# A macaron trunk in hi/lo fp32: the seven-product scheme moved from the down projection to gate and up

## The chip, the cores and the metric

One core of one Trainium2 chip runs the whole network in one program. The metric is the device time of one execution in microseconds, the median of three runs. Engines by their names in the profile: PE (matmul), ACT, DVE, POOL, and SP, which issues the DMAs.

## The reference, cut to what matters

```python
T, D, DFF = 512, 1024, 2816
def _swiglu(x, w_in, w_out):
    gate, up = jnp.split(x @ w_in, 2, axis=-1)
    return (jax.nn.silu(gate) * up) @ w_out
...
for layer in range(2):
    x = x + 0.5 * _swiglu(_rmsnorm(x, ffn1_norm[layer]), ffn1_w_in[layer], ffn1_w_out[layer])
    x = x + mixer(_rmsnorm(x, mix_norm[layer]))
    x = x + 0.5 * _swiglu(_rmsnorm(x, ffn2_norm[layer]), ffn2_w_in[layer], ffn2_w_out[layer])
return _rmsnorm(x, final_norm)
```

The mixer of layer 0 is a convolution beside sparse attention, that of layer 1 a short convolution beside stick-breaking attention. The change does not touch the mixers. Four FFNs (the `_swiglu` lines) are what it is about.

## The kernel before, in words

Tokens stay on chip as `xT`, 8 tiles of 128 channels x 512 tokens. Every fp32 operand is cut in two fp32r parts by `split`: ACT copies it to the high half, DVE subtracts to get the low half. `mm3` then makes three matmuls of each product: high weight by high tokens (L120), high weight by low tokens (L121), low weight by high tokens (L122). So PE cannot begin a weight before ACT's part is done, and its third matmul waits for DVE's. A weight tile is 128 x 1024; `load_w` brings it by one DMA of 512 KB, and the halves go to the pools `whi` and `wlo` with three slots each.

In an FFN, DFF is 22 blocks of 128. `up(s)` computes the gate and up projections of two blocks directly: four weights, 24 matmuls of 512 columns each into banks `gu`. The tokens are not normed ahead (the gain is in them, L94); DVE multiplies gate (L263) and up (L266) by `rstd`, ACT takes Silu, DVE multiplies both (L270). `rstd` itself is made while the first projections run: PE sums squares (`rs`, L187), DVE takes the inverse root, PE spreads it over the partitions (`rb`, L208), ACT copies it (L209).

`seven` is a scheme of seven block products in place of eight (Winograd's form of Strassen's). The 2 x 2 blocks are weights 11, 12, 21, 22 and the token operand in 2 x 2 blocks, with 256 token columns in a block. Sums of weight blocks come from DVE, sums of token blocks from DVE once per operand (`Seven`). In the kernel before, the down projection of 18 blocks goes this way: three groups of three pairs, two halves of the output channels each, that is six sevens per FFN of 7 x 18 matmuls of 256 columns. The products 11, T2, T1 and 22 add up in bank X (`px`), 12 in Y (`py`), T3 and T4 in W (`pw`), and after each product DVE adds the bank to `xT` (L285). The other four blocks go the direct way at the end (`down_tail`, 96 matmuls of 512 columns).

Order: each engine runs its instructions in a fixed order which a scheduler made when the kernel was built, and waits on semaphores. Names below end in numbers that count tiles.

Of the kernel before, what the change touches and what calls it, by code (L numbers as in the profile page):

```python
# [34 lines left out]
S_11, S_21, S_22, S_T1, S_T3, S_T2, S_T4 = 1, 2, 3, 4, 5, 6, 7  # L35


CHUNKS = [3, 3, 3]
TAIL = NP - 2 * sum(CHUNKS)

# [12 lines left out]
def trunk(ctx: ExitStack, tc: tile.TileContext, a: dict, out: bass.AP):  # L53
# [71 lines left out]
    def halves(t):  # L125
        return t.rearrange("p (s t) -> p s t", t=TH)

    def sums(e, b, t):

        x = [b[:, i * TH:(i + 1) * TH] for i in range(4)]  # L130
        y = [t[:, i * TH:(i + 1) * TH] for i in range(4)]
        e.tensor_tensor(y[0], x[1], x[0], ALU.subtract)
        e.tensor_tensor(y[1], x[3], x[0], ALU.subtract)
        e.tensor_tensor(y[2], x[3], y[0], ALU.add)
        e.tensor_tensor(y[3], y[2], x[2], ALU.subtract)

    class Seven:


        def __init__(self, hi, lo, b, t, e):  # L140
            self.hi, self.lo = hi, lo
            sums(e, b, t)
            split(hi[:, :3 * TH], lo[:, :3 * TH], b[:, TH:])
            split(hi[:, 3 * TH:], lo[:, 3 * TH:], t)

        def __getitem__(self, s):
            sl = slice((s - 1) * TH, s * TH)
            return self.hi[:, sl], self.lo[:, sl]


    class Norm:
        def __init__(self, col):
            self.col, self.h, self.l, self.ss, self.order = col, {}, {}, [], []

        def operand(self, k):
            hi = xnp.tile([P, T], F32R, tag="xn", name=nm("xh"))
            lo = xnp.tile([P, T], F32R, tag="xn", name=nm("xl"))
            split(hi, lo, xT[:, k, :], prm[:, self.col + k:self.col + k + 1])
            self.h[k], self.l[k] = hi, lo
            self.order.append(k)  # L160

        def square(self, k):
            sq = cp.tile([P, T], F32, tag="c", name=nm("sq"))
            S.activation(sq, xT[:, k, :], AF.Square)  # L164
            self.n = len(self.ss) and self.n + 1
            if not self.ss:
                self.ss = [sq]
            else:
                s2 = cp.tile([P, T], F32, tag="c", name=nm("ss"))
                (V if self.n == KD - 1 else G).tensor_tensor(s2, self.ss[0], sq, ALU.add)  # L170
                self.ss = [s2]
# [40 lines left out]
    def seven(ph, blocks, n, ops, taps):  # L212

        w = 2 * n * P
        raw = {}
        for b in ("11", "12", "22", "21"):
            raw[b] = ph.tile("rb", "rb", 768)[:, :w]
            nc.sync.dma_start(raw[b], blocks[b])  # L220
        s = {i: ph.tile("ws", "ws", 768)[:, :w] for i in (1, 2)}
        X, Y, W = (ph.bank(t, t) for t in ("px", "py", "pw"))

        def product(name, o, src, op, first, sign=None):
            hi = wsp.tile([P, 1024], F32R, tag="whi", name=nm("whi"))[:, :w]
            lo = wsp.tile([P, 1024], F32R, tag="wlo", name=nm("wlo"))[:, :w]
            split(hi, lo, src, sign)
            for k in range(n):
                for j in range(2):
                    sl = slice((j * n + k) * P, (j * n + k + 1) * P)  # L230
                    mm3(o[:, j * TH:(j + 1) * TH], hi[:, sl], lo[:, sl], *ops[k][op],
                        first and k == 0 and j == 0, k == n - 1, skip_group_check=True)
            taps(name, o)

        product("1", X, raw["11"], S_11, True)
        product("2", Y, raw["12"], S_21, True)
        V.tensor_tensor(s[1], raw["21"], raw["22"], ALU.add)
        V.tensor_tensor(s[2], s[1], raw["11"], ALU.add)
        product("6", X, s[2], S_T2, False, -1.0)
        V.tensor_tensor(raw["21"], raw["11"], raw["21"], ALU.add)  # L240
        product("7", W, raw["21"], S_T3, True)
        product("5", X, s[1], S_T1, False)
        product("4", W, raw["22"], S_T4, False)
        V.tensor_tensor(s[2], s[2], raw["12"], ALU.add)
        product("3", X, s[2], S_22, False)

    def ffn(norm, w_in, w_out, w_tail, nxt, ph, last=None):
        act = {}

        def up(s):  # L250

            blk = ph.wide("hb")
            for r in range(2):
                ps = []
                for gu in range(2):
                    hi, lo = load_w(w_in[2 * s + r, :, gu], KD * P)
                    o = ph.bank("gu")
                    for i, k in enumerate(norm.order):
                        sl = slice(k * P, (k + 1) * P)
                        mm3(o, hi[:, sl], lo[:, sl], norm.h[k], norm.l[k], i == 0, i == KD - 1)  # L260
                    ps.append(o)
                g = ph.tile("g")
                V.tensor_tensor(g, ps[0], rstd, ALU.mult)  # L263
                S.activation(g, g, AF.Silu)
                u = ph.tile("u")
                V.tensor_tensor(u, ps[1], rstd, ALU.mult)  # L266

                o = halves(blk)[:, 2 * r:2 * r + 2]
                tail = s >= sum(CHUNKS)
                V.tensor_tensor(o if r or tail else o[:, ::-1], halves(g), halves(u), ALU.mult)  # L270
            if tail:
                h, l = (ph.rtile("at", "act", 1792) for _ in range(2))
                split(h[:, :1024], l[:, :1024], blk)
                act[s] = [(h[:, r * T:(r + 1) * T], l[:, r * T:(r + 1) * T]) for r in range(2)]
                return
            act[s] = Seven(ph.rtile("ah", "act", 1792), ph.rtile("al", "act", 1792), blk, ph.wide("ht"), V)

        def down(c0, n, q):

            m0 = 4 * q  # L280

            def taps(m, o):
                r, c = {"1": (0, 0), "2": (0, 0), "6": (1, 0), "7": (1, 1), "5": (1, 1), "4": (1, 0), "3": (0, 1)}[m]
                x = xT[:, m0 + 2 * r:m0 + 2 * r + 2, c * TH:(c + 1) * TH]
                V.scalar_tensor_tensor(x, halves(o), -0.5 if r else 0.5, x, op0=ALU.mult, op1=ALU.add)  # L285

            w = 2 * n * P
            blocks = {b: w_out[q, i, :, 2 * c0 * P:2 * c0 * P + w] for i, b in enumerate(("11", "21", "12", "22"))}
            seven(ph, blocks, n, [act[c0 + k] for k in range(n)], taps)

        done = 0
        for i, n in enumerate(CHUNKS):
            c0 = sum(CHUNKS[:i])

            while done < min(c0 + n + 1, NP // 2):
                up(done)
                done += 1
            for q in range(2):
                down(c0, n, q)
                if done < NP // 2 and q == 0:  # L300
                    up(done)
                    done += 1

        ops = sum([act[s] for s in range(sum(CHUNKS), NP // 2)], [])
        ws = {}

        def down_tail(m, ts):
            o = ph.bank("fo")[:, ts]
            if m // 2 not in ws:
                ws[m // 2] = load_w(w_tail[m // 2], 2 * TAIL * P)  # L310
            hi, lo = ws[m // 2]
            for k in range(TAIL):
                sl = slice((m % 2 * TAIL + k) * P, (m % 2 * TAIL + k + 1) * P)
                mm3(o, hi[:, sl], lo[:, sl], ops[k][0][:, ts], ops[k][1][:, ts], k == 0, k == TAIL - 1)
            V.scalar_tensor_tensor(xT[:, m, ts], o, 0.5, xT[:, m, ts], op0=ALU.mult, op1=ALU.add)
# [20 lines left out]
    class Phase:  # L336
# [706 lines left out]
```

## Time and profile before

| | us |
|---|---|
| median of 3 runs | 1965.54 (1963.14 to 1967.5) |
| profiled execution | 1965.56 |
| its span in the trace | 1963.8 |
| mean granted clock of PE | 0.994 |

The profile is of one execution. Its span is 1.8 us shorter than the time of that execution, and that execution is within 0.1 us of the median, so rows of the trace can be added to the time directly.

### The profile page before, as it was taken

The page shows a single profiled execution, that of the slowest core. Times are in us where ns is not written, and L with a number is a line of the kernel's source. Part 1 is how long each engine was busy: PE and PEld are TensorE (multiplying, and loading weights), DVE is VectorE, ACT ScalarE, POOL GpSimd, SP SyncE. Part 2 cuts the span into 40 slices and gives each one's busy share as a digit, 9 for nine tenths or more (in the row PEclk, how much of TensorE's full clock was granted, in tenths as well). Part 3 has the DMA queues.
Part 4 walks back from the last instruction along what each step waited for, and adds up shares of the span by engine and source line. Part 5 has one row for each costly group of instructions (what it writes and reads, how often), then busy time and mean ns, then how long its engine had stood idle before and what let it go on. Part 6 is the DMA issues. An engine that isn't in the chain of part 4 may idle for free.

```text
span 1963.8 us, 25263 instructions
## 1 busy us (share of the span) xinstructions
PE 1930.6 (98%) x10128; PEld 1632.0 (83%) x10128; DVE 1322.0 (67%) x1973; ACT 790.1 (40%) x1129; POOL 104.1 (5%) x112
## 2 busy tenths in 40 slices
PE   8999999989999999999999999999999999999997
PEld 6888989878667888888988888888877888888896
DVE  6566757699986656666675666656578655666664
ACT  5333323436685433333343333334545433333333
POOL 2000000100232100000010000001000110000001
PEclk9999999999999999999999999999999999999999
DMA  6233331332100432323233333322321243232311
GB/s 220 94 91 102 92 102 52 100 103 82 43 1 28 150 97 84 113 82 117 86 111 96 97 97 98 98 80 75 94 67 55 77 143 97 84 114 81 117 52 54
DMA packets 53972, 178.02 MB, mean 91 GB/s; under 512 B 5984, under 2 KB 6368, under 8 KB 53856
## 3 DMA queue, kind: packets, MB, share of 16 engines
q1 hardware_dynamic: 53712, 176.29, 28.7%
q8 instruction: 79, 1.29, 0.3%
q14 instruction: 37, 0.30, 0.0%
q10 hardware_dynamic: 144, 0.14, 0.0%
HBM read 174.30 MB, written 2.10 MB: 90 GB/s over the span
## 4 chain that ended last, share of the span: by engine, by line
PE 97%; DVE 1%; ACT 1%; issue 0%; DMA 0%; DVEq 0%; SPq 0%; ACTq 0%
PE gu L120 16%; PE gu L121 16%; PE gu L122 16%; PE px L120 4%; PE px L122 4%; PE px L121 4%; PE ac L120 3%; PE ac L122 3%; PE ac L121 3%; PE pw L122 2%; PE pw L121 2%; PE pw L120 2%; PE fo L120 2%; PE fo L121 2%; PE fo L122 2%; PE mo L121 1%
## 5 line engine op out<-in xcount | busy, mean ns | idle before, releaser
L120 PE MATMUL gu<-xh,whi 128*128 128x512 f32 x1408 | 549.7, 391 | 8.3 <-ACT whi L90 6.1
L121 PE MATMUL gu<-xl,whi 128*128 128x512 f32 x1408 | 549.9, 391 | 0.0
L122 PE MATMUL gu<-xh,wlo 128*128 128x512 f32 x1408 | 546.4, 390 | 0.0
L90 ACT ACTIVATE whi<-raw 128x1024 fp32r<-128x1024 f32 (+2 forms) x256 | 268.9, 1051 | 565.3 <-PE gu L121 188.7
L91 DVE TENSOR_TENSOR wlo<-raw,whi 128x1024 fp32r<-128x1024 f32 (+2 forms) x256 | 312.8, 1222 | 55.0 <-ACT whi L90 51.0
L120 PEld LDWEIGHTS gu<-xh,whi 128*128 128x128 f32 x1408 | 265.5, 189 | 62.6 <-ACT whi L90 6.3
L122 PEld LDWEIGHTS gu<-xh,wlo 128*128 128x128 f32 x1408 | 265.2, 188 | 55.4
L121 PEld LDWEIGHTS gu<-xl,whi 128*128 128x128 f32 x1408 | 265.4, 189 | 53.8
L266 DVE TENSOR_TENSOR u<-gu,rstd 128x512 f32<-128x512 f32 x88 | 60.8, 691 | 264.6 <-PE gu L122 264.6
L90 ACT ACTIVATE whi<-rb 128x768 fp32r<-128x768 f32 x96 | 81.4, 848 | 266.5 <-PE gu L121 166.3
L263 DVE TENSOR_TENSOR g<-gu,rstd 128x512 f32<-128x512 f32 x88 | 60.8, 691 | 162.3 <-PE gu L122 155.8
L120 PE MATMUL px<-ah,whi 128*128 128x256 f32 x576 | 165.4, 287 | 1.6
L122 PE MATMUL px<-ah,wlo 128*128 128x256 f32 x576 | 163.4, 284 | 0.0
L121 PE MATMUL px<-al,whi 128*128 128x256 f32 x576 | 162.7, 282 | 0.0
L120 PEld LDWEIGHTS px<-ah,whi 128*128 128x128 f32 x576 | 108.8, 189 | 10.4 <-DVE xT L285 4.7
L120 PE MATMUL ac<-xh,whi 128*128 128x512 f32 x288 | 113.6, 395 | 1.5 <-ACT whi L90 1.5
L122 PE MATMUL ac<-xh,wlo 128*128 128x512 f32 x288 | 113.0, 393 | 0.0
L121 PE MATMUL ac<-xl,whi 128*128 128x512 f32 x288 | 112.8, 392 | 0.0
L121 PEld LDWEIGHTS px<-al,whi 128*128 128x128 f32 x576 | 108.7, 189 | 1.2
L122 PEld LDWEIGHTS px<-ah,wlo 128*128 128x128 f32 x576 | 108.6, 188 | 0.0
L170 POOL TENSOR_TENSOR ss<-sq,sq 128x512 f32<-128x512 f32 x7 | 12.5, 1787 | 1580.7 <-ACT sq L164 1580.7
L91 DVE TENSOR_TENSOR wlo<-rb,whi 128x768 fp32r<-128x768 f32 x96 | 91.7, 955 | 0.8
(316 smaller groups left out, 3245.8 us busy)
## 6 DMA issues: line engine op xcount, KB each, us to landing
raw<-in_w_in SPq DMA_DIRECT2D x174, 512.0 KB, 3.8
rb<-in_w_out SPq DMA_DIRECT2D x96, 384.0 KB, 3.1
raw<-in_cd_a SPq DMA_DIRECT2D x20, 512.0 KB, 3.6
raw<-in_w_tail SPq DMA_DIRECT2D x16, 512.0 KB, 4.0
raw<-in_ab_a SPq DMA_DIRECT2D x16, 512.0 KB, 3.5
raw<-in_ab_w_out SPq DMA_DIRECT2D x8, 512.0 KB, 3.7
raw<-in_cd_w_out SPq DMA_DIRECT2D x8, 512.0 KB, 3.6
xT<-in_x SPq DMA_DIRECT2D x8, 256.0 KB, 5.5
```

The source lines that it names most:

```text
L90: S.activation(hi, src, AF.Copy)
L91: V.tensor_tensor(lo, src, hi, ALU.subtract)
L120: PE.matmul(o, wh, xh, start=start, stop=False, **kw)
L121: PE.matmul(o, wh, xl, start=False, stop=False, **kw)
L122: PE.matmul(o, wl, xh, start=False, stop=stop, **kw)
L170: (V if self.n == KD - 1 else G).tensor_tensor(s2, self.ss[0], sq, ALU.add)
L263: V.tensor_tensor(g, ps[0], rstd, ALU.mult)
L266: V.tensor_tensor(u, ps[1], rstd, ALU.mult)
```

## The change

Gate and up of two of the eleven pairs stay direct (`DIRECT = 2`, so four blocks, eight weights). The other nine pairs go by seven block products each: the 2 x 2 weight blocks are gate and up by the two halves of the channels, each 512 channels x 256 outputs of the pair (eight tiles of 128 x 128, so 1024 columns wide on chip), and the tokens come in halves of 256. For that the tokens' operands have to be normed beforehand, since a product's sum is taken before the gate's Silu: `operands(i)`, four times per FFN, multiplies `xT` by gain and `rstd`, takes four sums and splits 7 x 256 columns into `x7`. The partial sums in bank X are copied out by ACT (L268: g0, u0, u1) between products, since X goes on adding. The down projection becomes direct: three groups of 7, 8 and 7 blocks, 24 weights per FFN of 21 or 24 matmuls of 512 columns; the first two groups are put between the sevens, up to three weights behind a seven.

```diff
+DIRECT = 2
+
+CHUNKS = [7, 8, 7]
...
-    def seven(ph, blocks, n, ops, taps):
...
-        def up(s):
...
-        def down(c0, n, q):
...
+    def ffn(norm, w_dir, w_in, w_out, nxt, ph, last=None):
+        act = []
+        HK = KD // 2
+
+        def act_tile():
+
+            n = len(act)
+            if CHUNKS[0] <= n < NP - CHUNKS[-1]:
+                act.append(tuple(xtile("act") for _ in range(2)))
+            else:
+                act.append(tuple(ph.rtile("act", "act", T) for _ in range(2)))
+            return act[-1]
+
+        def direct(p_):
+
+            ps = []
+            tag = ("b", "px", "pw")[p_ % 3]
+            for gu in range(2):
+                hi, lo = load_w(w_dir[p_, :, gu], KD * P)
+                o = ph.bank("gu", tag)
+                for k in range(KD):
+                    sl = slice(k * P, (k + 1) * P)
+                    mm3(o, hi[:, sl], lo[:, sl], norm.h[k], norm.l[k], k == 0, k == KD - 1)
+                ps.append(o)
+            g = ph.tile("g")
+            V.tensor_tensor(g, ps[0], rstd, ALU.mult)
+            S.activation(g, g, AF.Silu)
+            u = ph.tile("u")
+            V.tensor_tensor(u, ps[1], rstd, ALU.mult)
+            V.scalar_tensor_tensor(u, u, -1.0, g, op0=ALU.mult, op1=ALU.mult)
+            split(*act_tile(), u)
+
+        ops = []
+
+        def operands(i):
+
+
+            b, t = (ph.tile("xb", "rb", 1024) for _ in range(2))
+            for r in range(2):
+                k, o = i + r * HK, halves(b)[:, 2 * r:2 * r + 2]
+                V.scalar_tensor_tensor(o if r else o[:, ::-1], halves(xT[:, k, :]), norm.gain(k), halves(rstd),
+                                       op0=ALU.mult, op1=ALU.mult)
+            x = [b[:, j * TH:(j + 1) * TH] for j in range(4)]
+            y = [t[:, j * TH:(j + 1) * TH] for j in range(4)]
+            V.tensor_tensor(y[0], x[1], x[0], ALU.subtract)
+            V.tensor_tensor(y[1], x[3], x[0], ALU.subtract)
+            V.tensor_tensor(y[2], x[3], y[0], ALU.add)
+            V.tensor_tensor(y[3], y[2], x[2], ALU.subtract)
+            hi, lo = (ph.rtile("x7", "x7", 7 * TH) for _ in range(2))
+            split(hi[:, :3 * TH], lo[:, :3 * TH], b[:, TH:])
+            split(hi[:, 3 * TH:], lo[:, 3 * TH:], t)
+            ops.append((hi, lo))
+
+        def seven(s):
+
+
+            raw = {}
+            for n, b in enumerate(("11", "12", "22", "21")):
+                raw[b] = ph.tile("rb", "rb", 1024)
+                nc.sync.dma_start(raw[b], w_in[s, n])
+            ws = [ph.tile("ws", "ws", 1024) for _ in range(2)]
+            X, Y, W = (ph.bank(t, t) for t in ("px", "py", "pw"))
+            h = [ph.tile("h") for _ in range(2)]
+
+            def product(o, src, op, first, sign=None):
+                hi = wsp.tile([P, 1024], F32R, tag="whi", name=nm("whi"))
+                lo = wsp.tile([P, 1024], F32R, tag="wlo", name=nm("wlo"))
+                split(hi, lo, src, sign)
+                os = slice(op * TH, (op + 1) * TH)
+                for k in range(HK):
+                    for j in range(2):
+                        sl = slice((j * HK + k) * P, (j * HK + k + 1) * P)
+                        mm3(o[:, j * TH:(j + 1) * TH], hi[:, sl], lo[:, sl], ops[k][0][:, os], ops[k][1][:, os],
+                            first and k == 0 and j == 0, k == HK - 1, skip_group_check=True)
+
+            def copy(o):
+                c = ph.tile("c")
+                S.activation(c, o, AF.Copy)
+                return c
+
+            def out(c, g, u):
+
+                for j in range(2):
+                    js = slice(j * TH, (j + 1) * TH)
+                    V.tensor_tensor(h[j][:, c * TH:(c + 1) * TH], g[:, js], u[:, js], ALU.mult)
+
+            product(X, raw["11"], S_11, True)
+            g0 = copy(X)
+            product(Y, raw["12"], S_21, True)
+            V.tensor_tensor(g0, Y, g0, ALU.add)
+            S.activation(g0, g0, AF.Silu)
+            V.tensor_tensor(ws[0], raw["21"], raw["22"], ALU.add)
+            V.tensor_tensor(ws[1], ws[0], raw["11"], ALU.add)
+            product(X, ws[1], S_T2, False, -1.0)
+            u0 = copy(X)
+            V.tensor_tensor(raw["21"], raw["11"], raw["21"], ALU.add)
+            product(W, raw["21"], S_T3, True)
+            product(X, ws[0], S_T1, False)
+            u1 = copy(X)
+            V.tensor_tensor(u1, W, u1, ALU.add)
+            product(W, raw["22"], S_T4, False)
+            V.tensor_tensor(u0, W, u0, ALU.add)
+            out(0, g0, u0)
+            V.tensor_tensor(ws[1], ws[1], raw["12"], ALU.add)
+            product(X, ws[1], S_22, False)
+            S.activation(g0, X, AF.Silu)
+            out(1, g0, u1)
+            for x in h:
+                split(*act_tile(), x)
+
+        def down(m, c0, n, ts, end):
+            o = ph.bank("fo")[:, ts]
+            hi, lo = load_w(w_out[m, :, c0 * P:(c0 + n) * P], n * P)
             for k in range(n):
...
+                sl = slice(k * P, (k + 1) * P)
+                mm3(o, hi[:, sl], lo[:, sl], act[c0 + k][0][:, ts], act[c0 + k][1][:, ts], k == 0, k == n - 1)
+            V.scalar_tensor_tensor(xT[:, m, ts], o, -0.5, xT[:, m, ts], op0=ALU.mult, op1=ALU.add)
+
+        for p_ in range(2 * DIRECT):
+            direct(p_)
+            if p_ == 0:
+                for i in range(HK):
+                    operands(i)
+        ahead = []
+        s, i = DIRECT, 0
+        while s < NP // 2 or i < len(CHUNKS):
+            if s < NP // 2:
+                seven(s - DIRECT)
+                s += 1
             c0 = sum(CHUNKS[:i])
...
+            if not ahead and i < len(CHUNKS) - 1 and 2 * s >= c0 + CHUNKS[i] + 2:
+                ahead = [(m, c0, CHUNKS[i]) for m in range(KD)]
+                i += 1
+            for m, c0, n in ahead[:3]:
+                down(m, c0, n, slice(0, T), False)
+            del ahead[:3]
...
-        return Phase(dict(F=3, d=6, act=10, rb=6, ws=2), "b", b=4, px=1, py=1, pw=1, n=1)
+        return Phase(dict(x7=8, act=14, rb=4, ws=2, d=6), "b", b=2, px=2, py=1, pw=2, n=1)
```

PE at the hand-over from T1 to the last product. Before, in the first FFN's first down half: `px_149` under `whi_160` is T1, `pw_151` under `whi_162` is T4, `gu_170` the next projection, `px_149` under `whi_164` the last product.

```order
L120 MATMUL px_149_807<-ah_116_638,whi_160_905 128x256
L121 MATMUL px_149_807<-al_117_639,whi_160_905 128x256
L122 MATMUL px_149_807<-ah_116_638,wlo_161_906 128x256
L120 MATMUL pw_151_809<-ah_68_342,whi_162_928 128x256
...
L122 MATMUL pw_151_809<-ah_116_638,wlo_163_929 128x256
L120 MATMUL gu_170_982<-xh_7_94,whi_168_978 128x512
L121 MATMUL gu_170_982<-xl_8_95,whi_168_978 128x512
L120 MATMUL px_149_807<-ah_68_342,whi_164_952 128x256
L121 MATMUL px_149_807<-al_69_343,whi_164_952 128x256
L122 MATMUL px_149_807<-ah_68_342,wlo_165_953 128x256
```

After, in a seven of the first FFN with down weights behind it: `px_225` under `whi_240` is T1, `fo_251` is a down product, `px_225` under `whi_245` the last product.

```order
L120 MATMUL px_225_1360<-x7_73_327,whi_240_1486 128x256
L121 MATMUL px_225_1360<-x7_74_328,whi_240_1486 128x256
L122 MATMUL px_225_1360<-x7_73_327,wlo_241_1487 128x256
L120 MATMUL fo_251_1588<-act_57_273,whi_253_1591 128x512
L121 MATMUL fo_251_1588<-act_58_274,whi_253_1591 128x512
L120 MATMUL px_225_1360<-x7_61_285,whi_245_1549 128x256
L121 MATMUL px_225_1360<-x7_62_286,whi_245_1549 128x256
L122 MATMUL px_225_1360<-x7_61_285,wlo_246_1550 128x256
```

T4 moved from ahead of the last product to behind it; two matmuls of the filler are all that is left between.

ACT at the same places. Before:

```order
L90 ACTIVATE whi_160_905<-ws_147_805 128x768
L90 ACTIVATE whi_162_928<-rb_145_801 128x768
L90 ACTIVATE ah_140_786<-ht_142_788 128x1024
L90 ACTIVATE whi_164_952<-ws_148_806 128x768
L90 ACTIVATE whi_168_978<-raw_167_976 128x1024
L90 ACTIVATE whi_172_1009<-raw_171_1007 128x1024
L90 ACTIVATE whi_178_1046<-raw_177_1044 128x1024
```

After: the two L268 rows from `px_225` are the copies u0 (`c_237`) and u1 (`c_242`).

```order
L90 ACTIVATE whi_240_1486<-ws_223_1358 128x1024
L281 ACTIVATE c_232_1393<-c_232_1393 128x512
L90 ACTIVATE whi_243_1517<-rb_221_1354 128x1024
L268 ACTIVATE c_237_1455<-px_225_1360 128x512
L90 ACTIVATE whi_245_1549<-ws_224_1359 128x1024
L90 ACTIVATE whi_253_1591<-raw_252_1589 128x896
L268 ACTIVATE c_242_1514<-px_225_1360 128x512
L90 ACTIVATE whi_257_1620<-raw_256_1618 128x896
```

Behind the last product's high half (`whi_245`) stands the filler's (`whi_253`), and only then the copy u1 out of X. The slots of `whi` go round: 240, 243, 245, then 253 in the slot of 240.

DVE in the second FFN, from `rstd` on. Before, the first rows that use it:

```order
L263 TENSOR_TENSOR g_975_5857<-gu_970_5801,rstd_78 128x512
L266 TENSOR_TENSOR u_976_5860<-gu_974_5832,rstd_78 128x512
L263 TENSOR_TENSOR g_985_5925<-gu_980_5869,rstd_78 128x512
L91 TENSOR_TENSOR wlo_997_5977<-raw_995_5974,whi_996_5976 128x1024
L270 TENSOR_TENSOR hb_966_5794<-g_975_5857,u_976_5860 128x2x256
L132 TENSOR_TENSOR ht_989_5933<-hb_966_5794 128x256
L266 TENSOR_TENSOR u_986_5928<-gu_984_5900,rstd_78 128x512
L270 TENSOR_TENSOR hb_966_5794<-g_985_5925,u_986_5928 128x512
```

After, the last rows of the 51 from `g_1002`, the first that uses `rstd`, to `wlo_1070`, the low half of the first seven's first weight:

```order
L238 TENSOR_TENSOR xb_1015_6283<-xb_1015_6283,xb_1014_6282 128x256
L91 TENSOR_TENSOR act_1045_6451<-u_1043_6447,act_1044_6450 128x512
L237 TENSOR_TENSOR xb_1019_6297<-xb_1018_6296,xb_1019_6297 128x256
L219 TENSOR_TENSOR u_1055_6519<-gu_1053_6491,rstd_78 128x512
L238 TENSOR_TENSOR xb_1019_6297<-xb_1019_6297,xb_1018_6296 128x256
L91 TENSOR_TENSOR x7_1017_6291<-xb_1015_6283,x7_1016_6290 128x1024
L220 SCALAR_TENSOR_TENSOR u_1055_6519<-u_1055_6519,g_1054_6516 128x512
L91 TENSOR_TENSOR x7_1021_6305<-xb_1019_6297,x7_1020_6304 128x1024
L91 TENSOR_TENSOR wlo_1070_6542<-rb_1058_6526,whi_1069_6541 128x1024
L91 TENSOR_TENSOR act_1057_6523<-u_1055_6519,act_1056_6522 128x512
L91 TENSOR_TENSOR wlo_1073_6572<-rb_1059_6528,whi_1072_6571 128x1024
```

Before, DVE's rows behind `rstd` belonged to the projections; now the sums and low halves of all four operands (`xb`, `x7`) stand ahead of that weight's low half.

## Rows read from the trace of the kernel before

**Rows 1.** page of before, part 1 (busy us, share, instructions) and part 4 (chain)

```profile
PE 1930.6 (98%) x10128; PEld 1632.0 (83%) x10128; DVE 1322.0 (67%) x1973; ACT 790.1 (40%) x1129; POOL 104.1 (5%) x112
...
PE 97%; DVE 1%; ACT 1%; issue 0%; DMA 0%; DVEq 0%; SPq 0%; ACTq 0%
```

**Rows 2.** windows: length, busy time of each engine (instructions), granted clock, DMA share, GB/s

```profile
28.00:34.00 6.00, 4.51 (x23) 3.37 (x22) 4.52 (x16) 2.22 (x3) 0.00 (x0) 1.00 0.56 166
34.00:40.00 6.00, 5.27 (x16) 4.18 (x17) 5.88 (x12) 2.79 (x5) 0.00 (x0) 0.72 0.28 98
520.00:540.00 20.00, 18.62 (x86) 12.43 (x85) 18.05 (x50) 12.50 (x32) 7.32 (x13) 1.00 0.18 53
656.75:1012.41 355.66, 355.27 (x1922) 307.90 (x1920) 234.98 (x309) 126.56 (x148) 7.24 (x5) 1.00 0.34 104
```

**Rows 3.** timeline of PE: start, us, engine, line, operation

```profile
59.63 0.39 PE L120 MATMUL gu<-xh,whi 128*128 128x512 f32 x1
...
76.86 0.39 PE L121 MATMUL gu<-xl,whi 128*128 128x512 f32 x1
...
103.94 0.28 PE L120 MATMUL py<-ah,whi 128*128 128x256 f32 x1
...
110.30 0.29 PE L122 MATMUL pw<-ah,wlo 128*128 128x256 f32 x1
```

**Rows 4.** timeline, first FFN, sums of squares to the first use of rstd

```profile
27.44 0.95 PE L187 MATMUL rs<-ones,ss 128*128 128x1 f32 x8
...
31.89 0.62 PE L208 MATMUL rb<-cst,rcol 128*128 128x128 f32 x4
...
32.72 0.58 ACT L209 ACTIVATE rstd<-rb 128x512 f32<-128x512 f32 x1
...
34.73 0.50 PE L120 MATMUL gu<-xh,whi 128*128 128x512 f32 x1 [2.22 <-DVE g L263]
```

**Rows 5.** timeline of PE, a down projection by sevens, from T1 to the last product

```profile
112.78 0.28 PE L122 MATMUL px<-ah,wlo 128*128 128x256 f32 x1
...
115.04 0.39 PE L120 MATMUL gu<-xh,whi 128*128 128x512 f32 x1
...
115.53 0.39 PE L120 MATMUL px<-ah,whi 128*128 128x256 f32 x1
```

**Rows 6.** groups by line and form: busy us, mean ns, idle before and releasers

```profile
L90 ACT ACTIVATE whi<-raw 128x1024 fp32r<-128x1024 f32 x249 | 263.9, 1061 | 558.1 <-PE gu L121 188.7 <-issue 174.8 <-PE px L121 74.0
...
L90 ACT ACTIVATE th<-pt 128x512 fp32r<-128x512 f32 x48 | 27.9, 597 | 18.2 <-PE pt L394 17.8
```

**Rows 7.** timeline, a split of ACT and the matmul that it waits for

```profile
31.34 0.39 PE L121 MATMUL gu<-xl,whi 128*128 128x512 f32 x1
...
31.76 1.06 ACT L90 ACTIVATE whi<-raw 128x1024 fp32r<-128x1024 f32 x1 [5.33 <-PE gu L121]
```

**Rows 8.** timeline of DVE in the second FFN, and one row of the first

```profile
659.00 0.75 DVE L94 SCALAR_TENSOR_TENSOR xl<-xT,prm,xh 128x512 fp32r<-128x512 f32 x1
...
663.75 0.95 DVE L240 TENSOR_TENSOR rb<-rb,rb 128x768 f32<-128x768 f32 x1
...
664.69 1.22 DVE L91 TENSOR_TENSOR wlo<-raw,whi 128x1024 fp32r<-128x1024 f32 x1
665.82 0.17 DVE L192 TENSOR_SCALAR ri<-rv 128x4 int32<-128x4 int32 x1
...
674.16 0.69 DVE L263 TENSOR_TENSOR g<-gu,rstd 128x512 f32<-128x512 f32 x1 [3.23 <-ACT rstd L209]
674.77 0.68 DVE L266 TENSOR_TENSOR u<-gu,rstd 128x512 f32<-128x512 f32 x1
...
105.98 0.42 DVE L134 TENSOR_TENSOR ht<-hb,ht 128x256 f32<-128x256 f32 x1
```

**Rows 9.** page of before, part 6: DMA issues, KB each, us to landing

```profile
raw<-in_w_in SPq DMA_DIRECT2D x174, 512.0 KB, 3.8
```

**Rows 10.** timeline of PE in the first mixer

```profile
536.34 1.12 PE L684 MATMUL pm<-cc,ones 128*128 128x512 f32 x2 [1.38 <-DVE cc L465]
```

More of the change, by code (lines that the diff above doesn't have):

```diff
@@ L32 @@
 OFFT = [0, 512, 1024, 896]
-S_11, S_21, S_22, S_T1, S_T3, S_T2, S_T4 = 1, 2, 3, 4, 5, 6, 7
-CHUNKS = [3, 3, 3]
-TAIL = NP - 2 * sum(CHUNKS)
+S_11, S_21, S_22, S_T1, S_T3, S_T2, S_T4 = range(7)
+DIRECT = 2
+CHUNKS = [7, 8, 7]
 FILL = [3, 1, 1, 2, 1, 1, 2, 1]
@@ L122, in mm3, with gain @@
         PE.matmul(o, wl, xh, start=False, stop=stop, **kw)
[L125 to L148, printed above, removed]
     class Norm:
         def __init__(self, col):
-            self.col, self.h, self.l, self.ss, self.order = col, {}, {}, [], []
+            self.col, self.h, self.l, self.ss = col, [], [], []
+        def gain(self, k):
+            return prm[:, self.col + k:self.col + k + 1]
         def operand(self, k):
@@ L158, in operand @@
             split(hi, lo, xT[:, k, :], prm[:, self.col + k:self.col + k + 1])
-            self.h[k], self.l[k] = hi, lo
-            self.order.append(k)
+            self.h.append(hi)
+            self.l.append(lo)
         def square(self, k):
@@ L164, in square @@
             S.activation(sq, xT[:, k, :], AF.Square)
-            self.n = len(self.ss) and self.n + 1
-            if not self.ss:
+            if k == 0:
                 self.ss = [sq]
@@ L169, in square @@
                 s2 = cp.tile([P, T], F32, tag="c", name=nm("ss"))
-                (V if self.n == KD - 1 else G).tensor_tensor(s2, self.ss[0], sq, ALU.add)
+                (V if k == KD - 1 else G).tensor_tensor(s2, self.ss[0], sq, ALU.add)
                 self.ss = [s2]
@@ L209, in rsqrt_rows @@
         S.activation(row, pr[:, :nt * P], AF.Copy)
-    def seven(ph, blocks, n, ops, taps):
[L216 to L227, printed above, removed]
-            for k in range(n):
[L229 to L245, printed above, removed]
@@ L247, in ffn @@
-    def ffn(norm, w_in, w_out, w_tail, nxt, ph, last=None):
-        act = {}
-        def up(s):
[L252 to L276, printed above, removed]
-        def down(c0, n, q):
[L280 to L292, printed above, removed]
-            c0 = sum(CHUNKS[:i])
[L295 to L315, printed above, removed]
@@ new lines, in halves @@
+    def halves(t):
+        return t.rearrange("p (s t) -> p s t", t=TH)
+    def ffn(norm, w_dir, w_in, w_out, nxt, ph, last=None):
[94 more added lines that the diff above has]
+            hi, lo = load_w(w_out[m, :, c0 * P:(c0 + n) * P], n * P)
+            for k in range(n):
+                sl = slice(k * P, (k + 1) * P)
[12 more added lines that the diff above has]
+                s += 1
+            c0 = sum(CHUNKS[:i])
+            if not ahead and i < len(CHUNKS) - 1 and 2 * s >= c0 + CHUNKS[i] + 2:
[4 more added lines that the diff above has]
+            del ahead[:3]
+            if s == NP // 2 and i == len(CHUNKS) - 1 and not ahead:
+                break
+        c0, n = NP - CHUNKS[-1], CHUNKS[-1]
@@ L317, in ffn @@
         cut = KD - 1 if last else KD
         for m in range(cut):
-            down_tail(m, slice(0, T))
+            down(m, c0, n, slice(0, T), True)
             nxt(m)
@@ L323, in ffn @@
                 for m in range(cut, KD):
-                    down_tail(m, slice(c * TH, (c + 1) * TH))
+                    down(m, c0, n, slice(c * TH, (c + 1) * TH), True)
                 last(c, range(cut, KD))
@@ L329, in proj @@
         with when():
-            for i, k in enumerate(norm.order):
+            for k in range(KD):
                 sl = slice(k * P, (k + 1) * P)
-                mm3(o, hi[:, sl], lo[:, sl], norm.h[k], norm.l[k], i == 0, i == KD - 1)
+                mm3(o, hi[:, sl], lo[:, sl], norm.h[k], norm.l[k], k == 0, k == KD - 1)
     ph_ = [None]
@@ L860, in early_w @@
         sl = slice(c * T, (c + 1) * T)
-        nc.sync.dma_start(first[n][:, sl], a["w1_in"][0][0, :, n, sl])
+        nc.sync.dma_start(first[n][:, sl], a["w1_dir"][0][0, :, n, sl])
         return sp[n][0][:, sl], sp[n][1][:, sl], first[n][:, sl]
@@ L917, in last @@
             for b in range(2):
-                pt = ph.bank("ft")
+                pt = ph.bank("ft", ("px", "pw")[b])
                 for m in range(4):
@@ L937, in trunk @@
         n6.finish(lambda s: ph.bank(s, "n"))
-        ffn(n6, a["w2_in"][1], a["w2_out"][1], a["w2_tail"][1], nf_add, ph, last)
+        ffn(n6, a["w2_dir"][1], a["w2_in"][1], a["w2_out"][1], nf_add, ph, last)
 def _layout(i):
```

23 lines of the change are left out of this document (9 added, 14 removed).

## The prediction

> **What bounds the kernel now.** I read the page's busy times and its chain first, then the windows of one FFN, then the timeline at the places that the change rewrites. TensorE is busy 1930.6 of 1963.8 us and holds 97% of the chain that ended last [rows 1]. The second FFN's window says it more sharply: PE is busy 355.27 of 355.66 us, at granted clock 1.00 [rows 2]. Inside an FFN nothing but PE's own columns sets the time, so the change has to be counted twice: the columns it saves, and each place where PE, which now never waits there, would wait.
>
> **Columns.** The pitch of 512-column matmuls is (76.86 - 59.63)/76 = 0.2267 us and that of 256-column ones (110.30 - 103.94)/53 = 0.1200 [rows 3]: two halves cost 0.240, not 0.227. Per FFN before: 1056 (gate and up) + 96 (tail) = 1152 of 512 columns and 6 x 7 x 18 = 756 of 256. After: 192 (four direct blocks, eight weights) + 528 (down) = 720 of 512 and 9 x 7 x 24 = 1512 of 256. That is 432 x 0.2267 = 97.9 less and 756 x 0.12 = 90.7 more, so -7.2 per FFN and **-28.9** for four.
>
> The Trainium skill, "TensorE: Matmul & The Clock Gate", section "Back-to-back issue gap", gives N/2.4 + 2.5 ns between isolated matmuls, so 109 ns at 256 columns and 216 at 512, which by estimate would save 10.7 per FFN and 43 in all, and end 14 us lower than my sum. This trace's pitches are 10 and 5% longer than that, and the narrow matmul loses more, so I go by the rows.
>
> **The wait in the first FFN that goes.** PE waits 2.22 us for bank space behind the broadcast of rstd and resumes at 34.73 [rows 4]; the next window has granted clock 0.72 over 6 us [rows 2], which is 0.28 x 6 = 1.7 us lost. After the change the direct part has two banks under each of three tags, six projections fit before the first is read, and no bank is missing: **-3.9**.
>
> **Hand-over between the fifth and the last product, in each of 36 sevens.** Before, 18 matmuls of T4 into `pw` (to 115.04) and two of `gu` stood between the last matmul of T1 into `px` (112.78) and the last product into `px` (115.53), and PE never stopped: 115.04 + 2 x 0.2267 is 115.49 [rows 5]. Now T4 comes after the last product, and only two matmuls of another weight stand between. The last product adds onto bank X, so it must wait until ACT has copied X to u1 (L268). By ACT's order that copy stands behind the high half of the filler's weight, which needs the third slot of `whi`, the one that T1's second-last matmul frees. So the two ACT instructions run one after the other once T1 is over: split 1.06, PSUM copy 0.60 [rows 6]. ACT started 0.03 us after the matmul that it waited for (31.34 + 0.39 to 31.76) [rows 7]. Counted from the time at which PE could start the next matmul: -0.24 for the second-last matmul's start, its 0.28, 0.03 to ACT, 0.97 for the split (1.06 less an estimated 0.09 of overlap), 0.60, some 0.08 back to PE: 1.72, and 1.61 for a weight of 896 columns (128 fewer at (1061 - 597)/512 ns). Of it the filler's two matmuls cover 0.45 (512 columns) or 0.24 (256). Per FFN three sevens have a down weight of 896 (1.16), three one of 1024 (1.27), three the next seven's first product (1.48): 11.7 per FFN, **+46.9** in all, 1.30 each. Lower bound: the copy and all hand-offs cost no more than 1.43 and always 0.45 is covered, 0.98 each, 35. Upper: the fillers cover nothing, 1.72 each, 62. I take the middle, because both durations are rows of the same operation and shape.
>
> **The joint from the direct blocks to the first seven, once per FFN.** Every operand of the sevens is built from rstd by DVE. In the second FFN, from rstd's first use to the low half of the first seven's first weight, DVE's order holds 51 instructions: 15 of 512 columns, 8 of 512 with a column scalar, 16 of 256, 4 of 768, 8 of 1024. By the timeline each begins 0.08 or 0.09 us before the one ahead ends (0.69 gives 0.61, 1.22 gives 1.13) [rows 8], so 0.60, 0.67, 0.34, 0.87 and 1.13: 9.0 + 5.4 + 5.4 + 3.5 + 9.0 = 32.3. The first use stands at 674.16, 17.4 after the FFN's start; matmul counts ahead of rstd are those of before. So the low half is there at 17.4 + 32.3 + 0.1 = 49.8. PE has left the direct part at 192 x 0.2267 + 0.8 (sums of squares) + 0.45 (broadcast; the two are busy 0.95 and 0.62, less an estimated 0.15 that the next matmul overlaps) = 44.8 [rows 4], and has four matmuls more (0.5) that need only high halves. It waits 4.5 us; three FFNs, 13.5.
>
> In the first FFN rs starts at 27.44 after 81 matmuls [rows 4]; now after 85, at 28.35, and rb 32 matmuls later, at 28.35 + 0.8 + 7.25 = 36.4. rstd begins 0.83 behind (31.89 to 32.72) and takes 0.58 [rows 4], so DVE starts at 37.9. There 49 instructions stand ahead, 29.5 us by the same pitches: 67.5. PE is through at 28.35 + 0.8 + 107 x 0.2267 + 0.45 = 53.9, plus 0.24: it waits 13.4. Sum 26.9. Lower end: just that. Upper: whole durations rather than pitches, 0.085 x 51 = 4.3 more each, 44.
>
> After each joint I expect the clock loss seen after the 2.22 wait, 1.8 x 4 = 7: **+34.1** with it; bounds 27 to 51.
>
> **Costs of nothing.** DVE's work per seven: 11 of 1024, 5 of 512, 4 of 256 columns, 16.8 us, beside 168 x 0.12 = 20.2 of PE; without that cover it would be the bound. The DMA of four blocks of 512 KB, 3.8 us each to landing [rows 9], is issued one seven ahead. T4's bank is read while the last product runs. Down products are the former tail's form. If their cover fails, each is a rival below.
>
> **Sum.** Profiled execution 1965.56 (the median of the runs is 1965.54): 1965.6 - 28.9 - 3.9 + 46.9 + 34.1 = 2013.8. I say **2014**.
>
> **Rivals.** (1) The hand-over is hidden: copy and split fall under PE's work, as DVE's tap on T1 did before [rows 5]. Then 1965.6 - 32.8 + 34.1 = 1967, no change, and without a clock loss at the joints 1965.6 - 32.8 + 27 = 1960, faster. With joints of 27 it is faster by over 4 us as long as a hand-over costs under 0.05 us, and slower by as much from 0.27 on. Against it: only two matmuls lie between, and ACT runs in order. 0.06 (0.04 faster, 0.02 same).
>
> (2) The clock falls at hand-overs too. For: after 2.22 us of waiting it did [rows 2, 4]. Against: a wait of 1.38 at 536.34 left 520 to 540 at 1.00 [rows 2, 10]. If at each, 36 x 1.7 = 61 more, 2075; if at a third, 2034, still in the range. 0.08 for more than half of them.
>
> (3) DVE or the weights' DMA is late in the three sevens in a row without down products: DVE has 3.4 us of slack in 20.2. It would add to waits that are there already, some 10 to 20: 2030. 0.05, within the range.
>
> (4) The change does not do what it says, since narrow matmuls eat the saving: four weight blocks cost 4 x 0.2267 = 0.907 us direct and 7 x 0.12 = 0.840 by sevens [rows 3]. A saving of 7% is left of the nominal 12.5, so this holds in part and is in the sum already.
>
> **How the numbers follow.** Main forecast 0.81; its own range is 1965.6 - 32.8 + 35 + 27 = 1995 to 1965.6 - 32.8 + 62 + 51 = 2046. With rival 3 it holds 0.86. Rival 1 lies below, rival 2 above. I set the range at 1992 to 2046. A measurement of this kernel can tell about 0.2%, 4 us, from no change: faster 0.04, same 0.02, slower 0.94.
>
> **What would show it.** Right: PE waits of 1 to 1.5 us for ACT's copy or for the filler's split, 36 times; in the windows of the three later FFNs PE idles about 12 + 5 us where it idled 0.4; one wait near 54 us of some 13; the low half of the first product named as releaser. The 512 and 256 pitches unchanged. Wrong: the last product following T1 without a gap; a clock under 0.9 through the sevens; PE waiting on DMA. If DVE is busy over 95% of a seven, rival 3 holds.

## The result, and the profile after

| | us |
|---|---|
| changed kernel, median of 4 runs | 2017.86 (2016.57 to 2019.39) |
| kernel before, median of 4 runs | 1965.56 (1963.14 to 1967.5) |
| ratio | 1.0267, 95% interval 1.0249 to 1.0285 |
| span of the profiled execution | 2015.5 (before 1963.8) |

The change makes the kernel 2.7% slower, 52 us. The forecast was 2014 in a range of 1992 to 2046.

The page of the changed kernel, parts 1 and 4, answers to [rows 1]:

```profile
PE 1920.5 (95%) x11433; PEld 1675.3 (83%) x11433; DVE 1386.2 (69%) x1966; ACT 899.8 (45%) x1298; POOL 110.4 (5%) x112
...
PE 91%; DVE 4%; ACT 3%; DMA 1%; issue 1%; DVEq 0%; SPq 0%; ACTq 0%
```

PE is busy 10 us less, although 2.7% more time passes, and its share of the last chain fell from 97 to 91%: what came in between are ACT, DVE and a little DMA. The windows of the second and third FFN answer to the last row of [rows 2] (length, busy time of PE, PEld, DVE, ACT and POOL, granted clock, DMA):

```profile
677.91:1045.15 367.24, 352.77 (x2246) 318.64 (x2244) 248.16 (x305) 155.11 (x192) 10.04 (x6) 0.99 0.31 95
1045.15:1413.75 368.60, 352.80 (x2245) 318.69 (x2244) 247.88 (x305) 153.51 (x191) 10.05 (x6) 0.99 0.31 95
```

PE idles 14.5 us in the second FFN where it idled 0.4. The view of PE's waits says for whom (sum, times, longest):

```profile
PE px L120 <- ACT whi L90: 37.9, 16, 14.1
PE fo L120 <- ACT whi L90: 23.9, 24, 1.1
...
PE py L120 <- ACT whi L90: 6.2, 3, 2.3
```

Nearly all of it is for ACT's high half of a weight: 24 times about 1 us ahead of a down product, 12 times ahead of the next seven's first product, and the long ones at the joints. One hand-over in the timeline, from the last matmul of T1 to the first of the last product (PE and ACT):

```profile
132.75 0.28 PE L122 MATMUL px<-x,wlo 128*128 128x256 f32 x1
133.01 0.95 ACT L90 ACTIVATE whi<-raw 128x896 fp32r<-128x896 f32 x1 [1.79 <-PE px L121]
...
133.87 0.58 ACT L268 ACTIVATE c<-px 128x512 f32<-128x512 f32 x1
134.01 0.50 PE L120 MATMUL fo<-act,whi 128*128 128x512 f32 x1 [0.98 <-ACT whi L90]
134.35 0.40 PE L121 MATMUL fo<-act,whi 128*128 128x512 f32 x1
134.59 0.30 PE L120 MATMUL px<-x,whi 128*128 128x256 f32 x1
```

The split waits for T1's second-last matmul (L121), the copy stands right behind the split, PE stands 0.98 us for the split, and the last product begins 0.14 us after the copy's end (133.87 + 0.58). Without waits it would begin at 132.75 + 0.12 + 2 x 0.2267 = 133.32, so this hand-over costs 1.27. Worked out so, all 36 lie between 1.20 and 1.49 and add up to 48.0 us.

The joint of the second FFN, which starts at 677.91 (SP, ACT, PE and DVE):

```profile
721.84 5.46 SPq L250 DMA_DIRECT2D rb<-in_w_in  x4
...
725.31 1.06 ACT L90 ACTIVATE whi<-rb 128x1024 fp32r<-128x1024 f32 x1
...
726.42 0.58 PE L120 MATMUL px<-x,whi 128*128 128x256 f32 x1 [3.40 <-ACT whi L90]
...
726.86 1.22 DVE L91 TENSOR_TENSOR wlo<-rb,whi 128x1024 fp32r<-128x1024 f32 x1
...
728.06 1.06 ACT L90 ACTIVATE whi<-rb 128x1024 fp32r<-128x1024 f32 x1 [1.17 <-DMA rb<-in_w_in]
...
729.17 0.58 PE L120 MATMUL py<-x,whi 128*128 128x256 f32 x1 [1.96 <-ACT whi L90]
```

PE waits 3.40 + 1.96. DVE ends the first weight's low half at 728.08 (726.86 + 1.22), 50.2 us after the FFN's start. But what PE waits for last is the high half of the second weight, and that split waits for a weight that SP only began to fetch from 721.84 on. The view of SP's waits from 700 to 733 us names what held the fetch, the last sums of the operands (L238), which lie in the same slots `rb`:

```profile
SPq L250 <- DVE xb L238: 13.0, 2, 11.1
```

In the first FFN the wait is the longest of the kernel, and there even DVE stands for the first high half (SP, ACT, DVE and PE):

```profile
64.07 3.11 SPq L250 DMA_DIRECT2D rb<-in_w_in  x3
...
67.66 1.06 ACT L90 ACTIVATE whi<-rb 128x1024 fp32r<-128x1024 f32 x1 [2.57 <-DMA rb<-in_w_in]
...
68.74 1.23 DVE L91 TENSOR_TENSOR wlo<-rb,whi 128x1024 fp32r<-128x1024 f32 x1 [2.07 <-ACT whi L90]
...
68.76 0.58 PE L120 MATMUL px<-x,whi 128*128 128x256 f32 x1 [14.10 <-ACT whi L90]
```

### The profile page after: what moved, and what is told of

It reads as the page before. It is cut to its first block, busy times and chain, and to the rows that moved or that the text cites. A ratio compares the mean times of both kernels' runs of the same rounds, so it can differ in the third digit from the quotient of the medians.

```text
span 2015.5 us, 28053 instructions
## 1 busy us (share of the span) xinstructions
PE 1920.5 (95%) x11433; PEld 1675.3 (83%) x11433; DVE 1386.2 (69%) x1966; ACT 899.8 (45%) x1298; POOL 110.4 (5%) x112
## 4 chain that ended last, share of the span: by engine, by line
PE 91%; DVE 4%; ACT 3%; DMA 1%; issue 1%; DVEq 0%; SPq 0%; ACTq 0%
PE fo L120 8%; PE fo L121 8%; PE fo L122 8%; PE px L120 7%; PE px L121 7%; PE px L122 7%; PE pw L121 3%; PE pw L120 3%; PE pw L122 3%; PE ac L120 3%; PE ac L122 3%; PE ac L121 3%; PE gu L120 2%; ACT whi L90 2%; PE gu L122 2%; PE gu L121 2%
## 5 line engine op out<-in xcount | busy, mean ns | idle before, releaser
L90 ACT ACTIVATE whi<-raw 128x1024 fp32r<-128x1024 f32 (+3 forms) x193 | 195.0, 1011 | 476.5 <-issue 163.9
L120 PE MATMUL px<-x,whi 128*128 128x256 f32 x1152 | 332.1, 288 | 39.1 <-ACT whi L90 37.9
L121 PE MATMUL px<-x,whi 128*128 128x256 f32 x1152 | 328.4, 285 | 0.0
L122 PE MATMUL px<-x,wlo 128*128 128x256 f32 x1152 | 326.8, 285 | 0.5 <-DVE wlo L91 0.5
L120 PE MATMUL fo<-act,whi 128*128 128x512 f32 (+1 forms) x711 | 281.1, 395 | 23.9 <-ACT whi L90 23.9
L121 PE MATMUL fo<-act,whi 128*128 128x512 f32 (+1 forms) x711 | 278.0, 391 | 0.0
L122 PE MATMUL fo<-act,wlo 128*128 128x512 f32 (+1 forms) x711 | 277.9, 391 | 0.0
L91 DVE TENSOR_TENSOR wlo<-raw,whi 128x1024 fp32r<-128x1024 f32 (+3 forms) x193 | 225.5, 1169 | 69.9 <-ACT whi L90 66.0
L120 PEld LDWEIGHTS px<-x,whi 128*128 128x128 f32 x1152 | 221.0, 192 | 51.0 <-ACT whi L90 42.1
L121 PEld LDWEIGHTS px<-x,whi 128*128 128x128 f32 x1152 | 220.9, 192 | 0.8
L122 PEld LDWEIGHTS px<-x,wlo 128*128 128x128 f32 x1152 | 219.9, 192 | 0.9 <-DVE wlo L91 0.8
L120 PEld LDWEIGHTS fo<-act,whi 128*128 128x128 f32 x711 | 133.6, 188 | 56.1 <-ACT whi L90 28.8
L120 PE MATMUL pw<-x,whi 128*128 128x256 f32 x576 | 162.2, 282 | 0.7 <-ACT whi L90 0.7
L121 PE MATMUL pw<-x,whi 128*128 128x256 f32 x576 | 162.7, 282 | 0.0
L121 PEld LDWEIGHTS fo<-act,whi 128*128 128x128 f32 x711 | 133.7, 188 | 28.0
```

The lines of the kernel that those rows point to most:

```text
L90: S.activation(hi, src, AF.Copy)
L91: V.tensor_tensor(lo, src, hi, ALU.subtract)
L120: PE.matmul(o, wh, xh, start=start, stop=False, **kw)
L121: PE.matmul(o, wh, xl, start=False, stop=False, **kw)
L122: PE.matmul(o, wl, xh, start=False, stop=stop, **kw)
```

## The experiments

Times are medians against the kernel before on the same chip (1965.0 and 1965.1). "FFN 2" is the length of the second FFN, 355.66 before and 367.24 after the change. The first mixer, of which no run edits more than the pools that it takes its slots from (the fourth slot and the control for it), does not take the same time in all of these kernels, so the total alone misleads. From the profiled executions, in us, the fourth FFN counted to the end of the program:

| run | four FFNs | first mixer | granted clock in it |
|---|---|---|---|
| kernel before | 1455.8 | 286.6 | 0.98 |
| changed kernel | 1508.4 | 286.8 | 0.98 |
| T4 in a bank of its own | 1459.7 | 298.0 | 0.94 |
| a fourth slot for high halves | 1505.3 | 300.8 | 0.94 |
| the control for it | 1508.1 | 289.9 | 0.97 |
| three direct pairs | 1471.7 | 306.5 | 0.90 |
| both mends | 1429.1 | 287.0 | 0.98 |
| first weights early | 1519.5 | 296.8 | 0.93 |
| the same with T4's bank | 1471.0 | 291.5 | 0.96 |
| the copy u1 by DVE | 1561.3 | 292.1 | 0.96 |

**T4 in a bank of its own.**

```diff
-            X, Y, W = (ph.bank(t, t) for t in ("px", "py", "pw"))
+            X, Y, W, W4 = (ph.bank(t, t) for t in ("px", "py", "pw", "pw"))
...
-            product(W, raw["22"], S_T4, False)
             V.tensor_tensor(u0, W, u0, ALU.add)
+            product(W4, raw["22"], S_T4, True)
+            V.tensor_tensor(u0, W4, u0, ALU.add)
```

> T4 gets a bank of its own, so that it can stand between T1 and the last product again; DVE adds one bank more per seven (36 adds of 512 columns). Theory (the hand-over costs what ACT's split and copy take one after the other behind T1, 1.33 us each in the trace of the changed kernel): T4's 24 matmuls, 2.9 us, cover 1.7 us, the 36 hand-overs lose their 48 us, 1970 (1966 to 1976), and the waits at the four joints stay at 14 and 5 to 7 us. Rival (the wait only moves, since DVE then has 17.4 us of work in a seven of 20.2 and is late with low halves): 1990 to 2010, with DVE as the releaser of PE.

Measured: 1978.96, ratio 1.0069 (1.0054 to 1.0084); FFN 2 355.51, 11.7 less. PE's waits in the four FFNs are now these and 2.3 us of smaller ones in the first, all at the joints:

```profile
PE px L120 <- ACT whi L90: 25.7, 4, 14.1
PE py L120 <- ACT whi L90: 6.9, 3, 2.6
```

The 36 hand-overs are gone: 22 of T4's 24 matmuls now stand between T1 and the last product, and PE does not wait there. Nothing moved to DVE. The four FFNs together are 49 us shorter. The whole gained only 38.9, and the total lies above the theory's range, since the first mixer took 298.0 us where it took 286.8; more on that below.

**A fourth slot for high halves.** The pool of `whi` has four slots, that of raw weights two.

```diff
-    wraw = ctx.enter_context(tc.tile_pool(name="wraw", bufs=3))
+    wraw = ctx.enter_context(tc.tile_pool(name="wraw", bufs=2))
+    whp = ctx.enter_context(tc.tile_pool(name="whp", bufs=4))
...
-            hi = wsp.tile([P, 1024], F32R, tag="whi", name=nm("whi"))
+            hi = whp.tile([P, 1024], F32R, tag="whi", name=nm("whi"))
```

> A fourth slot for high halves of weights, paid for with the third slot of raw weights; T4 stays behind the last product and the copy stays where it is in the program. Theory with the slot as the root (the filler's split cannot run before T1 frees a slot, and the copy stands behind it): the split now runs under T1, the copy alone is 0.7 us and more filler matmuls fit ahead of the last product, so the hand-overs lose 40 to 48 us: 1970 to 1978. Rival (the copy out of X by itself is what the last product waits for): about 0.3 to 0.5 us per hand-over stay, 1982 to 1988.

Measured: 2028.75, ratio 1.0319 (1.0303 to 1.0334); FFN 2 368.64. Both readings fell. The timeline at a hand-over (T1's last matmul at 799.54):

```profile
799.42 0.28 PE L122 MATMUL px<-x,whi 128*128 128x256 f32 x1
...
799.66 0.39 PE L121 MATMUL fo<-act,whi 128*128 128x512 f32 x1
...
799.79 0.95 ACT L91 ACTIVATE whi<-raw 128x896 fp32r<-128x896 f32 x1 [1.89 <-DMA rb<-in_w_in]
...
800.65 0.58 ACT L269 ACTIVATE c<-px 128x512 f32<-128x512 f32 x1
...
800.80 0.50 PE L121 MATMUL fo<-act,whi 128*128 128x512 f32 x1 [0.51 <-ACT whi L91]
```

The first filler is split ahead of T1's end, but the order made for four slots puts a second filler's split ahead of the copy. That one begins 0.09 us after T1's second-last matmul ends (799.42 + 0.28), as in the changed kernel, so it waits for T1's slot again; the DMA that the view names fills `rb`, which this split does not read. The wait halves to 0.5 to 0.6 at the down products and new ones come: PE waits 15.7 us for `py`'s weight, where it waited 6.2, and 6.1 for low halves, where it waited 0.5. The four FFNs are 3 us shorter where 40 to 48 were expected; that the total is longer than the changed kernel's comes from the first mixer, 14 us longer. With three slots and with four, ACT's order runs one split further than there are slots.

**The control for it.** Only `wraw` from 3 to 2.

> Control for the four slots: only the third slot of raw weights is taken away. Theory: weights for the direct and down products land in time, 2018 with 36 hand-overs as before (2014 to 2024). Rival (two slots make the down weights late): 2030 or more, PE waiting for ACT's split that waits for a DMA.

Measured: 2018.26, ratio 1.0269 (1.0248 to 1.0289): the third raw slot is worth nothing here. The 10 us by which the run before is slower than this one are not in the FFNs, which are 2.8 us shorter there, but in the first mixer, 10.9 longer.

**Three direct pairs.** `DIRECT = 3`.

> Three pairs direct in place of two, eight sevens in place of nine per FFN. Theory (the joint waits for DVE's building of operands, which now has 21.8 us more of PE's direct work over it): 36 us of waits and some 6 us of half clock at the four joints go, a pair costs 21.8 direct and 20.2 plus 1.3 as a seven, so +1: about 1977 (1972 to 1984), 32 hand-overs of 1.33 stay. Rival (the first seven's weights are late because their slots are held by the operands' sums until the end, whatever stands before): the joints keep several us each, 1990 to 2000.

Measured: 1990.35, but in two groups, 2000.24 and 1999.25 with mean granted clock 0.982 and 1981.44 and 1981.06 with 0.992 and 0.993; ratio 1.0111 (1.0063 to 1.0159). In the profiled execution FFN 2 is 360.09. The waits for the first seven's weights at the joints are gone; the first FFN keeps 0.35 for a low half, 2.7 ahead of the third product and 0.6. The hand-overs stay:

```profile
PE fo L120 <- ACT whi L90: 23.9, 24, 1.1
PE px L120 <- ACT whi L90: 8.2, 8, 1.0
```

So 21.8 us more of direct work cover the joint: its end is set from `rstd` on, not from the end of the direct part. That fits the theory, but it does not part DVE's own sum from the fetch of the weights, since DVE's sums hold that too. The median lies in the rival's range by the first mixer alone, 306.5 us where it was 286.8; with 286.8 the profiled execution would be in the theory's range (2000.24 - 19.7 = 1980.5).

**Both mends.** T4's bank and `DIRECT = 3`.

> T4's own bank and three direct pairs together. Theory (columns as forecast, hand-overs and joints the only waits that the change brought): no wait of PE over 0.5 us inside the four FFNs but for the first FFN's start; the second FFN takes 816 x 0.2267 + 1344 x 0.12 + 1.25 = 347.5 us against 355.66 in the kernel before; with the first mixer at 287 to 306 us (its clock fell for 20 to 38 us in the last runs) the whole is 1929 to 1948, faster than the kernel before. Rival (narrow matmuls or DVE, with 17.4 us of work in a seven of 20.2, cost more once the waits are gone): the second FFN stays at 353 or above and the whole at 1955 or above.

Measured: 1944.30 (1938.21 to 1947.98), ratio 0.9886 (0.9866 to 0.9905): 1.1% faster than the kernel before, and the version to keep. Its second and third FFN:

```profile
652.85:1002.28 349.43, 349.43 (x2173) 315.31 (x2172) 243.22 (x305) 150.37 (x186) 10.05 (x6) 1.00 0.33 100
1002.28:1352.25 349.97, 349.62 (x2174) 315.23 (x2172) 243.60 (x305) 148.75 (x185) 10.05 (x6) 1.00 0.33 100
```

PE does not idle at all in the second; in the first, waits of 0.4, 2.7 and 0.6 us are left at the joint. 349.4 is 1.9 above the 347.5 from the pitches and 6.2 below the kernel before, so the columns' gain is real; by the pitches it is 5.6 with three direct pairs (351.9 to 346.3).

**The first seven's weights early.** One tile of each operand in the slots of the weight sums.

```diff
-            b, t = (ph.tile("xb", "rb", 1024) for _ in range(2))
+            b, t = ph.tile("xb", "ws", 1024), ph.tile("xt", "rb", 1024)
```

> The operands' tiles b lie in the two slots of the weight sums and only the tiles t in the four slots of the sevens' raw weights, so that the first seven's weights can land before the operands are finished; nothing else is changed. Theory as predicted (the joint waits for DVE's building of the operands): the first joint falls from 16.4 to about 13.4 us and the later ones from 5.4 to 6.7 to about 4.5, with DVE's low halves as the releaser: 2009 (2006 to 2014). Rival (the raw weights' DMA, held back until the operands' tiles are free, is what the joint waits for): the joints all but vanish, under 2 us each and 6 in the first FFN: 1990 to 1998. Third case: one operand at a time is slower, and the joints grow: over 2020.

Measured: 2035.04, ratio 1.0352 (1.0334 to 1.0370): the third case. In the second FFN the first two products start without a wait, but then PE stands 8.4 us ahead of the third, whose weight is a sum in the slots now held by operands and needs blocks that landed late:

```profile
PE px L120 <- ACT whi L93: 29.5, 4, 8.4
...
743.67 1.23 DVE L282 TENSOR_TENSOR ws<-rb,rb 128x1024 f32<-128x1024 f32 x1 [3.35 <-DMA rb<-in_w_in]
```

The wait moved on and grew in the three later FFNs (from 5.4 to 6.7 us up to 8.8 to 9.7); this does not part the DMA's share of the joint from DVE's, since DVE's order changed too. The four FFNs are 11 us longer, and the first mixer another 10.

**The same with T4's bank.**

> The tiles as in the run before, and T4's own bank. Theory: the two gains add, since one is at the joint and one inside the sevens: 1979 less 5 to 9 (1968 to 1975). Rival (joint limited by the DMA): 1955 to 1960.

Measured: 1981.44, ratio 1.0073 (1.0054 to 1.0092), with the same wait of up to 8.4 us ahead of the third product (29.0 in four FFNs). The placing costs 11 us in the four FFNs here too, against T4's bank alone; the totals, 1981.44 and 1978.96, hide it because the first mixer is 6.5 us shorter. So the joint is mended by work over it and not by this placing.

**The copy u1 by DVE.**

```diff
-            u1 = copy(X)
+            u1 = ph.tile("c")
+            V.tensor_copy(u1, X)
```

> The copy u1 out of X is made by DVE in place of ACT; order of PE and slots stay, so that the filler's split on ACT still waits for the slot that T1 frees. Theory (of a hand-over of 1.33 us the split with its slot is 1.1, the copy behind it only what the filler's two matmuls do not cover): hand-overs of 1.0 to 1.15, 6 to 12 us less in all, 2006 to 2012. Rival (the copy is what the last product waits for, the split would be covered): 0.3 each, 1980. Third case: DVE comes late to the copy because its lows stand ahead: no gain or slower.

Measured: 2073.39, ratio 1.0546 (1.0519 to 1.0572), the third case and much worse than it was priced. A hand-over (PE and DVE; T1's last matmul at 808.76):

```profile
809.57 1.22 DVE L282 TENSOR_TENSOR ws<-rb,rb 128x1024 f32<-128x1024 f32 x1 [1.09 <-DMA rb<-in_w_in]
810.72 0.68 DVE L290 COPY c<-px 128x512 f32<-128x512 f32 x1
...
810.02 0.50 PE L120 MATMUL fo<-act,whi 128*128 128x512 f32 x1 [0.98 <-ACT whi L90]
...
811.46 0.58 PE L120 MATMUL px<-x,whi 128*128 128x256 f32 x1 [0.71 <-DVE c L290]
811.83 0.42 PE L121 MATMUL px<-x,whi 128*128 128x256 f32 x1
```

The wait for the split stays (0.98). The copy stands on DVE behind a sum of the next seven's weights that itself waits for a DMA, and PE waits 29.3 us for it over 36 hand-overs. In 30 of them a filler stands between, and they cost 1.8 to 3.2 us each. In the other six the scheduler put no filler there, so that PE waits for the copy alone, and they cost 1.0. Behind the second wait above the next matmul takes 0.42 in place of 0.28: from 811.5 to 814.8 the granted clock is 0.50.

## Why the prediction held, step by step

**Columns, -28.9.** Held. Once the waits were mended, FFN 2 fell 6.2 below the kernel before, where the pitches gave 5.6 with three direct pairs.

**The wait in the first FFN, -3.9.** Held: no wait stands behind `rb` any more.

**Hand-overs, +46.9.** Held: 48.0, and by the steps named, split for the slot that T1's second-last matmul frees, then the copy. By kind 1.20 to 1.27 (forecast 1.16), 1.30 to 1.37 (1.27) and 1.43 to 1.49 (1.48). That T4 no longer stands between is shown as the cause by the first experiment, which put it back and took all 36 away. What the fourth slot and DVE's copy add: neither one slot more nor another engine for the copy takes the hand-over away. That ACT's order is to blame, with the split that needs T1's slot ahead of the copy, is read from the timelines; no run put the copy ahead of that split.

**Joints, +26.9 of waits.** The waits came and go back to DVE's sums of operands, but the term was too small, 33.9 (16.4, 5.4, 6.7, 5.4), and the releaser was not the one named. DVE ended the low half at 50.2 us where 49.8 was forecast, so its 51 instructions were counted rightly. But of the 33.9 PE waited only 0.5 for a low half, and the rest for ACT's high halves. The forecast put the weights' DMA among the costs of nothing, as issued one seven ahead; the first seven has no seven ahead of it. The operands' sums take the same four slots `rb` as the first seven's weights, so those DMAs began only at 721.84, and the high halves that end the wait came 1 to 2 us behind what DVE's sum alone gives. In the first FFN this put the first low half's start to 68.74 where 66.3 was counted. How much of the joint would be left to the DMA alone is open, since the experiment for it made a new wait.

**The clock after the joints, +7.** Near it: in the second FFN 14 matmuls from 729.55 on run at a pitch of 0.213 in place of 0.120, 1.3 us, and some 0.5 more at the two restarts, so 1.8 as forecast. The first FFN has two such stretches and loses some 3.8 by the same count, which makes about 9 in all.

**Sum.** 2014 and 2017.86. The four stages with FFNs, each from its first matmul, came out at +21.6, +11.6, +12.9 and +7.2 us, by the forecast's steps +15.8 and three times +10.8. The fourth is counted to the end of the program, which the forecast did not look at and where, among other things, a wait of PE for ACT went from 2.6 us down to 1.3. So that the sum is only 4 us short is partly luck: the joints and their clock cost 9 us more than forecast, and the last stage came out 3.6 lower.

**Rivals.** (1), a hidden hand-over, did not come. (2), the clock falling at hand-overs, did not come at 1.2 to 1.5 us, and came in the last experiment: with 30 hand-overs of 1.8 to 3.2 us the granted clock goes to 0.50 in 17 stretches outside the joints, each at one of them or within 2 us behind it. (3) did not come: DVE is not the bound in the sevens in a row, not even with one add more.

## What to carry to other kernels

When a scheme saves columns, count first where each product's bank is read and what then stands between that read and the next product into the bank: here some 22 matmuls of 256 columns in between, in each of 36 sevens, were worth 48 us, more than the columns saved. A split that must wait for a slot should not stand ahead of the copy that frees a bank on an engine that runs in order; here one slot more only moved that point. Work that can start only after a late scalar (rstd) needs as much independent work over it as its own engine's sum of durations.

## What the runs showed of the hardware that was not expected

The first mixer, whose code was not edited, took 286.6 us in the kernel before, 286.8 after the change, 298.0 with T4's bank and 306.5 with three direct pairs (the profiled executions); in the table above its time goes with the granted clock in it. Windows of 580 to 600 us (some 200 to 230 us behind the mixer's start) of the kernel before, of T4's bank and of three direct pairs:

```profile
580.00:600.00 20.00, 20.00 (x104) 13.63 (x104) 15.80 (x53) 16.77 (x48) 7.05 (x14) 1.00 0.00 1
```

```profile
580.00:600.00 20.00, 19.21 (x75) 12.21 (x75) 9.74 (x39) 10.06 (x29) 8.21 (x16) 0.70 0.00 0
```

```profile
580.00:600.00 20.00, 20.00 (x61) 13.14 (x60) 8.53 (x31) 10.00 (x28) 5.89 (x12) 0.50 0.01 1
```

In the last two the granted clock is at its lower level (1.2 of 2.4 GHz) for much or all of that stretch, although PE counts as busy for nearly all of it and its waits just before were no longer than those of the kernel before (at most 1.5 us). Executions of one and the same program differ too: with three direct pairs two runs took 2000 at a mean clock of 0.982 and two 1981 at 0.992 and 0.993, and with both mends the runs spread from 1938 at 0.993 to 1948 at 0.987. Only one execution of each kernel was traced, so that it is this stretch that comes and goes between them is likely but not shown. The order of the mixer's instructions is not the same in these kernels, since the scheduler makes it anew; it differs between the kernel before and the changed one too, where the clock in the mixer is the same. What decides the clock there is not settled. It is why gains inside the FFNs should be read from their windows.
